# Linear attention's heads: output with tokens on the partitions, normalised by row sums, transposed afterwards

## The chip, the core and the metric

The kernel runs on one core of a Trainium2 chip. The metric is the device time of one execution in microseconds, the median of the runs shown. Engines are named as in the profile: PE is TensorE's matmul stream and PEld its weight loads, DVE is VectorE, ACT is ScalarE, POOL is GpSimd, SP is SyncE, which issues the DMAs.

## What is computed

A sequence of 512 tokens with 1024 features goes through four layers: sparse attention with an MLP, a convolution mixer with an MLP, a layer with a gated recurrence and a short convolution, and a gated linear attention layer. The change lies in the last one. Cut to what matters there:

```python
def odd_layer(x, norm_pre, norm_post, w_in, w_gate_lr, b_gate, head_norm_g, w_out):
    h = rmsnorm_2(x, norm_pre)
    q, k, v, r, lr = jnp.split(h @ w_in, [512, 1024, 2048, 3072], axis=-1)
    ...
    o_f = gla_chunked(qh, kh, vh, g_f)
    o_b = jnp.flip(gla_chunked(jnp.flip(qh, 2), jnp.flip(kh, 2), jnp.flip(vh, 2), jnp.flip(g_b, 2)), 2)
    o = rmsnorm_2(o_f + o_b, head_norm_g)
    o = jnp.transpose(o, (0, 2, 1, 3)).reshape(bsz, seq, GLA_VAL)
    y = (o * jax.nn.silu(r.astype(jnp.float32))) @ w_out
    return (x + rmsnorm_2(y, norm_post)).astype(x.dtype)
```

There are four heads with keys of 128 and values of 256 features. Each head's output, 512 tokens by 256 features, is the sum of a forward and a backward pass. It is normalised over the 256 features of each token, multiplied by a gain per feature (`head_norm_g`) and by silu(r), and goes into the last matrix product.

## The kernel before, in words

All large products are made in three matmuls of a rounded high part and a rest (`XH`, `XL` for the activations, `whi`, `wlo` for the weights, all fp32r, 512 columns each; lines 145 to 147 in `mac`). Weights come in chunks of 128 x 1024 by DMA into `stg`; ACT makes `whi` (L99) and DVE makes `wlo` (L100).

In the last layer the work of the heads is cut into steps: the generator `head(hd)` issues a few instructions and yields. The foreground is the stream of matmuls for `r` (eight output tiles `m`, each 24 matmuls) and then for `wod`, the last product. After every six matmuls of `r`, or every three of `wod`, `step` lets the background go on; which generator goes next is set by their place in a list `bg`, by credits, and by conditions at which a generator yields `WAIT`. So the order on every engine is fixed when the kernel is built, and a generator with another number of yields shifts all that come after it. All engines take their instructions in that order. After each tile `m`, DVE makes `rz` (L1567), ACT its sigmoid `sr` (L1569), POOL their product (L1570), and PE transposes a tile of the residual `h` (`hT`, L1552), which ACT copies back (L1553).

A head goes through these stages: scores `gsc` (L1408), masked by DVE into `Sm` (L1409) and added by POOL into `Sc` (L1411); transposed keys `ktT` (L1423); three rounds of `kv` (L1435), each followed by two `Z` on DVE (L1442, L1445) and two `U` on ACT (L1448), which are the states; and then the output, which the change rewrites.

The output stands with features on the partitions. For each half `eh` of the 256 features, one PSUM tile `go` of 128 x 512 holds all four blocks of 128 tokens, in ten matmuls of 128 columns:

```python
pe.matmul(o[:, pp], lhsT=vS[:, p, ec], rhs=Sc[:, p, :], start=True, stop=False)
if p > 0:
    pe.matmul(o[:, pp], lhsT=U[0, p][:, eu], rhs=E[hd, 0][0][:, pp], start=False, stop=p == 3)
if p < 3:
    pe.matmul(o[:, pp], lhsT=U[1, p][:, eu], rhs=E[hd, 1][0][:, pp], start=False, stop=True)
```

ACT squares the finished tile (`osq`, `sq`), POOL adds the two halves (L260), PE sums over the partitions by matmuls with a column of 1/256 (`om`, L267), ACT and DVE make the reciprocal root `rh` (L282, L283), four transposes spread it over the partitions (`spread`, L272), ACT copies it to `ori` (L274), DVE multiplies it and the gain on (`on`, L1493), and POOL, for the last head DVE, multiplies by `sr` (L1499). Then `tosplit` makes `XH` (L297) and `XL` (L298) from it for `wod`. PSUM tiles have tags: `a` with two buffers (`go`), `b` with two (`gsc`, `ktT`, `kv`), `c` with one (`om`, `spread`), `mm` with three (`r`, `hT`, `wod`).

Of the kernel before, what the change touches and what calls it, by code (L numbers as in the profile page):

```python
# [45 lines left out]
def tile_model(ctx, tc, xT, wall, gwall, vecs, opost, wglr, bglr, wdw, dft, out):  # L46
# [25 lines left out]
    def psum(tag, name):  # L72
        n = {"mm": 3, "a": 2, "b": 2, "c": 1}[tag]
        return ps.tile([P, NT], F32, tag=tag, name=name, bufs=n)
# [122 lines left out]
    def V(name, i=0, n=1):  # L197
        o = VEC[name] + i
        return vec[:, o:o + n]
# [41 lines left out]
    def tmp(name="t"):  # L241
        return tmp_pool[0].tile([P, NT], F32, tag="t", name=name, bufs=tmp_pool[1])
# [11 lines left out]
    def add_sq(k, src, acc, scale=1.0, eng=pool):  # L254
        if k == 0:
            act.activation(acc, src, AF.Square, scale=scale)
        else:
            t = tmp("sq")[:, :src.shape[-1]]
            act.activation(t, src, AF.Square, scale=scale)  # L259
            eng.tensor_tensor(out=acc, in0=acc, in1=t, op=ALU.add)  # L260
# [4 lines left out]
    def means(m, acc, col, scale_col, js=range(4)):  # L265
        for j in js:
            pe.matmul(m[:, col + j:col + j + 1], lhsT=acc[:, j * P:(j + 1) * P], rhs=scale_col, start=True, stop=True)  # L267
# [11 lines left out]
    def rsqrt_cols(dst, src):  # L279
        s = small("sd")  # L280
        n = src.shape[-1]
        act.activation(s[:, :n], src, AF.Sqrt, bias=eps)  # L282
        dve.reciprocal(dst, s[:, :n])  # L283
# [989 lines left out]
    with eo as e:  # L1273
# [20 lines left out]
        for d in range(2):  # L1294
# [11 lines left out]
            t = gp.tile([P, 4, P], F32, name=f"Sm{d}")  # L1306
            pool.memset(t, 0.0)
            Sm.append(t)
        ones256 = gp.tile([P, 1], F32, name="ones256")
        pool.memset(ones256, 1.0 / 256)  # L1310

        lro = psum("mm", "lr")
        hi, lo = weights()
# [84 lines left out]
        def head(hd):  # L1398
            while len(live) == 2:
                yield WAIT  # L1400
            live.append(hd)
            U = {}
            for d in range(2):
                qt, kt = E[hd, d]
                s = psum("b", "gsc")
                for p in range(4):
                    pp = slice(p * P, (p + 1) * P)
                    pe.matmul(s[:, pp], lhsT=kt[:, pp], rhs=qt[:, pp], start=True, stop=True)  # L1408
                dve.copy_predicated(Sm[d], mk[d], s.rearrange("p (a b) -> p a b", a=4))  # L1409
            Sc = hp.tile([P, 4, P], F32, tag="Sc", name="Sc", bufs=2)  # L1410
            pool.tensor_tensor(out=Sc, in0=Sm[0], in1=Sm[1], op=ALU.add)  # L1411
            yield
            while kb:
                yield WAIT
            kb.append(hd)
            order = [list(range(3)), list(range(3, 0, -1))]
            kts = []
            for d in range(2):
                kt = E[hd, d][1]
                t = psum("b", "ktT")  # L1420
                for p in order[d]:
                    pp = slice(p * P, (p + 1) * P)
                    pe.transpose(t[:, pp], kt[:, pp], ident)  # L1423
                k_ = hp.tile([P, NT], F32, tag="kTs", name="kTs", bufs=3)
                sl = slice(0, 3 * P) if d == 0 else slice(P, 4 * P)
                act.activation(k_[:, sl], t[:, sl], AF.Copy)
                kts.append(k_)
            yield
            yield
            Z = [None, None]  # L1430
            for i in range(3):
                kp = psum("b", "kv")
                for d in range(2):
                    p = order[d][i]
                    pe.matmul(kp[:, d * 256:(d + 1) * 256], lhsT=kts[d][:, p * P:(p + 1) * P], rhs=vS[:, p, hd * 256:(hd + 1) * 256], start=True, stop=True)  # L1435
                for d in range(2):
                    p = order[d][i]
                    gm = gam[hd, d]
                    kd = kp[:, d * 256:(d + 1) * 256]
                    zt = hp.tile([P, 256], F32, tag="Z", name="Z", bufs=4)  # L1440
                    if i == 0:
                        dve.tensor_copy(zt, kd)  # L1442
                    else:
                        q = order[d][i - 1]
                        dve.scalar_tensor_tensor(zt, Z[d], gm[:, q:q + 1], kd, op0=ALU.mult, op1=ALU.add)  # L1445
                    Z[d] = zt
                    ut = hp.tile([P, 256], F32, tag="U", name="U", bufs=12)
                    act.activation(ut, zt, AF.Copy, scale=gm[:, p:p + 1])  # L1448
                    U[d, p + 1 if d == 0 else p - 1] = ut
                if i == 2:  # L1450
                    kb.clear()
                    kvd.append(hd)
                yield
            while busy:
                yield WAIT
            busy.append(hd)
            for _ in range(2 if hd == 3 else 0):
                yield
            os_ = []
            sq = tmp("osq")  # L1460
            for eh in range(2):
                o = psum("a", "go")
                ec = slice(hd * 256 + eh * P, hd * 256 + (eh + 1) * P)
                eu = slice(eh * P, (eh + 1) * P)
                for p in range(4):
                    pp = slice(p * P, (p + 1) * P)
                    pe.matmul(o[:, pp], lhsT=vS[:, p, ec], rhs=Sc[:, p, :], start=True, stop=False)
                    if p > 0:
                        pe.matmul(o[:, pp], lhsT=U[0, p][:, eu], rhs=E[hd, 0][0][:, pp], start=False, stop=p == 3)
                    if p < 3:  # L1470
                        pe.matmul(o[:, pp], lhsT=U[1, p][:, eu], rhs=E[hd, 1][0][:, pp], start=False, stop=True)
                add_sq(eh, o, sq)
                os_.append(o)
                if eh:
                    live.remove(hd)
                yield
            yield
            for _ in range(2 if hd == 3 else 0):
                yield
            m = psum("c", "om")  # L1480
            means(m, sq, 0, ones256)
            rh = small("rh")
            rsqrt_cols(rh, m[:, 0:4])
            yield
            ri = tmp("ori")
            spread(ri, rh)
            yield
            while 2 * hd + 1 not in sr:
                yield WAIT
            on = []  # L1490
            for eh in range(2):
                t = tmp("on")
                dve.scalar_tensor_tensor(t, os_[eh], V("glg", eh), ri, op0=ALU.mult, op1=ALU.mult)  # L1493
                on.append(t)
            busy.clear()
            yield
            for eh in range(2):
                m = 2 * hd + eh
                (dve if hd == 3 else pool).tensor_tensor(out=sr[m], in0=on[eh], in1=sr[m], op=ALU.mult)  # L1499
                done.append(m)  # L1500
            yield

        done = []
        kvd = []
# [314 lines left out]
```

## Time and profile before

| | us |
|---|---|
| median of 3 runs | 1816.83 |
| lowest and highest | 1815.49, 1822.7 |
| the profiled execution, its own time | 1816.9 |
| its span, first to last instruction | 1815.2 |
| PE busy | 1785.0 |
| DVE, ACT, POOL busy | 979.1, 815.7, 442.5 |

The span is what the profile covers; the 1.7 us around it belong to the start and the end of the execution. Matmuls overlap in the pipeline, so a row's duration of one is longer than what it costs in a stream of them; the chain of waits shows the latter.

### The profile page before, as it was taken

The numbers are of one execution on the slowest core, as the hardware profiler recorded it, in microseconds if no ns is written. First come the engines' busy times: TensorE is split into PE (matmuls) and PEld (weight loads), VectorE is DVE, ScalarE is ACT, GpSimd is POOL, SyncE is SP. The second block draws the span as 40 slices with busy tenths as digits, with TensorE's granted clock in tenths as the row PEclk, the third lists the DMA queues.
The fourth block names the chain that finished last, engine by engine and source line by source line (L and its number), as shares of the span: only waits on it lengthen the run. The fifth ranks groups of instructions, "written<-read, shape, count | busy, mean of one in ns | idle before, by whom it ended". The sixth has DMA issues, their size and how long they took to land.

```text
span 1815.2 us, 22602 instructions
## 1 busy us (share of the span) xinstructions
PE 1785.0 (98%) x8796; PEld 1490.1 (82%) x8796; DVE 979.1 (54%) x1430; ACT 815.7 (45%) x1267; POOL 442.5 (24%) x380
## 2 busy tenths in 40 slices
PE   9999999999999999999999999999999999999998
PEld 7778878888888878898888888888887888888887
DVE  4796544333333658765333333786677743756354
ACT  5334444332323434564332323558666734456553
POOL 1333422010202202436010202412313103552330
PEclk9999999999999999999999999999999999999999
DMA  5222113223232233112323222232322233222121
GB/s 191 70 71 81 47 59 104 94 93 104 93 104 93 82 103 105 47 40 78 105 93 104 87 100 94 81 116 95 100 96 76 91 112 104 72 99 70 47 71 47
DMA packets 45931, 159.68 MB, mean 88 GB/s; under 512 B 5217, under 2 KB 6625, under 8 KB 45824
## 3 DMA queue, kind: packets, MB, share of 16 engines
q1 hardware_dynamic: 45824, 158.24, 26.1%
q8 instruction: 69, 1.13, 0.3%
q14 instruction: 38, 0.31, 0.1%
HBM read 156.13 MB, written 2.10 MB: 87 GB/s over the span
## 4 chain that ended last, share of the span: by engine, by line
PE 88%; DVE 5%; ACT 3%; issue 2%; DMA 1%; POOL 0%; SPq 0%; DVEq 0%; ACTq 0%; POOLq 0%
PE w L146 12%; PE w L147 12%; PE w L145 12%; PE ko L146 2%; PE ko L147 2%; PE ko L145 1%; PE a L145 1%; PE a L147 1%; PE a L146 1%; PE k L145 1%; PE lg L467 1%; PE o L499 1%; ACT whi L99 1%; PE v L441 1%; PE q L147 1%
## 5 line engine op out<-in xcount | busy, mean ns | idle before, releaser
L100 DVE TENSOR_TENSOR wlo<-stg,whi 128x1024 fp32r<-128x1024 f32 x247 | 328.5, 1332 | 267.5 <-ACT whi L99 266.4
L99 ACT ACTIVATE whi<-stg 128x1024 fp32r<-128x1024 f32 x284 | 297.6, 1051 | 222.5 <-PE w L146 125.4
L596 POOL TENSOR_TENSOR UL<-u,UH 128x512 fp32r<-128x512 f32 x64 | 83.5, 1305 | 514.5 <-ACT UH L595 514.5
L145 PE MATMUL w<-XH,whi 128*128 128x512 f32 (+1 forms) x520 | 200.7, 386 | 0.0
L146 PE MATMUL w<-XL,whi 128*128 128x512 f32 (+1 forms) x520 | 200.7, 386 | 0.0
L147 PE MATMUL w<-XH,wlo 128*128 128x512 f32 (+1 forms) x520 | 200.7, 386 | 0.0
L146 PE MATMUL w<-UL,whi 128*128 128x512 f32 x512 | 199.5, 390 | 0.1
L147 PE MATMUL w<-UH,wlo 128*128 128x512 f32 x512 | 199.3, 389 | 0.0
L145 PE MATMUL w<-UH,whi 128*128 128x512 f32 x512 | 199.3, 389 | 0.0
L100 POOL TENSOR_TENSOR wlo<-stg,whi 128x1024 fp32r<-128x1024 f32 x37 | 89.6, 2428 | 122.1 <-ACT whi L99 121.9
L260 POOL TENSOR_TENSOR sacc<-sacc,sq 128x512 f32<-128x512 f32 (+1 forms) x57 | 71.0, 1253 | 182.4 <-ACT sq L259 118.3
L147 PEld LDWEIGHTS w<-XH,wlo 128*128 128x128 f32 x520 | 97.7, 188 | 19.7
L145 PEld LDWEIGHTS w<-XH,whi 128*128 128x128 f32 x520 | 97.7, 188 | 19.7
L146 PEld LDWEIGHTS w<-XL,whi 128*128 128x128 f32 x520 | 97.7, 188 | 19.6
L146 PEld LDWEIGHTS w<-UL,whi 128*128 128x128 f32 x512 | 96.1, 188 | 20.9 <-POOL UL L596 1.0
L145 PEld LDWEIGHTS w<-UH,whi 128*128 128x128 f32 x512 | 96.1, 188 | 20.0
L147 PEld LDWEIGHTS w<-UH,wlo 128*128 128x128 f32 x512 | 96.1, 188 | 19.9
L592 ACT ACTIVATE relu<-w 128x512 f32<-128x512 f32 x64 | 38.2, 597 | 151.8 <-PE w L147 151.8
L594 DVE TENSOR_TENSOR u<-relu 128x512 f32<-128x512 f32 x64 | 45.4, 709 | 104.5 <-ACT relu L592 104.5
L146 PE MATMUL ko<-XL,whi 128*128 128x256 f32 x256 | 74.6, 291 | 3.8 <-DVE XL L252 2.2
L145 PE MATMUL ko<-XH,whi 128*128 128x256 f32 x256 | 75.5, 295 | 2.4 <-ACT XH L823 2.4
L604 DVE TENSOR_TENSOR acc<-w,acc 128x512 f32<-128x512 f32 x32 | 22.1, 691 | 97.0 <-PE w L147 97.0
(485 smaller groups left out, 4101.1 us busy)
## 6 DMA issues: line engine op xcount, KB each, us to landing
stg<-wall SPq DMA_DIRECT2D x284, 512.0 KB, 3.3
gst<-gwall SPq DMA_DIRECT2D x4, 512.0 KB, 3.6
h<-xT SPq DMA_DIRECT2D x3, 512.0 KB, 6.2
out<-yo SPq DMA_DIRECT2D x6, 256.0 KB, 2.1
stg<-wall SPq DMA_DIRECT2D x8, 128.0 KB, 5.2
h<-xT SPq DMA_DIRECT2D x2, 256.0 KB, 4.1
ex<-wglr SPq DMA_DIRECT2D x2, 256.0 KB, 2.7
sacc<-opost SPq DMA_DIRECT2D x2, 256.0 KB, 4.4
```

What stands on the lines that cost most here:

```text
L99: act.activation(hi, src, AF.Copy)
L100: eng.tensor_tensor(out=lo, in0=src, in1=hi, op=ALU.subtract)
L145: pe.matmul(o, lhsT=hi[:, w], rhs=xh[:, k, ns], start=first, stop=False)
L146: pe.matmul(o, lhsT=hi[:, w], rhs=xl[:, k, ns], start=False, stop=False)
L147: pe.matmul(o, lhsT=lo[:, w], rhs=xh[:, k, ns], start=False, stop=last)
L260: eng.tensor_tensor(out=acc, in0=acc, in1=t, op=ALU.add)
L441: pe.matmul(acc[t], lhsT=XH[:, k, xs], rhs=wh, start=k == 0, stop=False)
L467: pe.matmul(l[:, :w], lhsT=qh[hd][:, j * P:(j + 1) * P], rhs=kT[:, hd, :w], start=True, stop=True)
L592: act.activation(r, o, AF.Relu)
L594: dve.tensor_tensor(out=u, in0=r, in1=r, op=ALU.mult)
L596: pool.tensor_tensor(out=UL[:, m, :], in0=u, in1=UH[:, m, :], op=ALU.subtract)
L604: dve.tensor_tensor(out=a, in0=o, in1=a, op=ALU.add)
```

## The change

The output of a head is now made with tokens on the partitions. For each block p of 128 tokens the operands change places: `Sc` and the decayed queries are the stationary ones, `vS` and `U` the moving ones with all 256 features, so a block is one product of 128 x 256. Blocks 0 and 1 lie side by side in one `go` tile, blocks 2 and 3 in another. ACT squares each block and sums along the row with it (`accum_out`), which gives `ss`; ACT takes the root and DVE the reciprocal (`rh`), and the four blocks are scaled by it into `on`, blocks 0 and 2 on ACT, 1 and 3 on DVE. Then, for each half of the features, PE transposes four times into a tile `onT` (tag `c`), and DVE multiplies by the gain and by `sr` in one instruction. The sums by POOL, `om`, `spread`, `ori` and the products on POOL are gone, and the yields of the generator stand at other places.

```diff
-            os_ = []
-            sq = tmp("osq")
-            for eh in range(2):
-                o = psum("a", "go")
-                ...
-                add_sq(eh, o, sq)
-                os_.append(o)
-                if eh:
-                    live.remove(hd)
-                yield
-            yield
-            for _ in range(2 if hd == 3 else 0):
-                yield
-            m = psum("c", "om")
-            means(m, sq, 0, ones256)
+            os_ = [psum("a", "go") for _ in range(2)]
+            ss = small("ss")
+            dv = slice(hd * 256, (hd + 1) * 256)
+            outs = [os_[p // 2][:, (p % 2) * 256:(p % 2) * 256 + 256] for p in range(4)]
+            for p in range(4):
+                pp = slice(p * P, (p + 1) * P)
+                o = outs[p]
+                pe.matmul(o, lhsT=Sc[:, p, :], rhs=vS[:, p, dv], start=True, stop=False)
+                if p > 0:
+                    pe.matmul(o, lhsT=E[hd, 0][0][:, pp], rhs=U[0, p], start=False, stop=p == 3)
+                if p < 3:
+                    pe.matmul(o, lhsT=E[hd, 1][0][:, pp], rhs=U[1, p], start=False, stop=True)
+                act.activation(tmp("osq")[:, :256], o, AF.Square, accum_out=ss[:, p:p + 1])
+                if p == 3:
+                    live.remove(hd)
+                if p % 2:
+                    yield
+            yield
             rh = small("rh")
-            rsqrt_cols(rh, m[:, 0:4])
-            yield
-            ri = tmp("ori")
-            spread(ri, rh)
+            act.activation(rh, ss, AF.Sqrt, scale=1.0 / 256, bias=eps)
+            dve.reciprocal(rh, rh)
+            on = [tmp("on") for _ in range(2)]
+            for p in range(4):
+                w = on[p // 2][:, (p % 2) * 256:(p % 2) * 256 + 256]
+                if p % 2:
+                    dve.tensor_scalar(w, outs[p], rh[:, p:p + 1], None, op0=ALU.mult)
+                else:
+                    act.activation(w, outs[p], AF.Copy, scale=rh[:, p:p + 1])
+            busy.clear()
             yield
             while 2 * hd + 1 not in sr:
                 yield WAIT
-            on = []
+            for _ in range(2 if hd == 3 else 1):
+                yield
             for eh in range(2):
-                t = tmp("on")
-                dve.scalar_tensor_tensor(t, os_[eh], V("glg", eh), ri, op0=ALU.mult, op1=ALU.mult)
-                on.append(t)
-            busy.clear()
-            yield
-            for eh in range(2):
+                t = psum("c", "onT")
+                for p in range(4):
+                    pe.transpose(t[:, p * P:(p + 1) * P], on[p // 2][:, (p % 2) * 256 + eh * P:(p % 2) * 256 + eh * P + P], ident)
                 m = 2 * hd + eh
-                (dve if hd == 3 else pool).tensor_tensor(out=sr[m], in0=on[eh], in1=sr[m], op=ALU.mult)
+                dve.scalar_tensor_tensor(sr[m], t, V("glg", eh), sr[m], op0=ALU.mult, op1=ALU.mult)
                 done.append(m)
-            yield
+                yield
```

Three places of the built order, each before and after; a bracket names the engines whose semaphores an instruction waits for. First PE at head 0's output, blocks of the first group (`vS` are the values, `Sc` the scores, `U` the states, `qk` and `qkb` the decayed queries forward and backward). Before:

```order
L1467 MATMUL go<-Sc,vS_12498 128x128 [waits Pool_49]
L1471 MATMUL go<-qkb_12441,U 128x128 [waits Activation_49]
L1467 MATMUL go<-Sc,vS_12498 128x128
L1469 MATMUL go<-qk_12440,U 128x128
L1471 MATMUL go<-qkb_12441,U 128x128
```

After, the same place, lines 1465 to 1469 of the changed kernel:

```order
L1465 MATMUL go<-vS_12498,Sc 128x256 [waits Pool_49]
L1469 MATMUL go<-U,qkb_12441 128x256 [waits Activation_49]
L1465 MATMUL go<-vS_12498,Sc 128x256 [waits Activation_49]
L1467 MATMUL go<-U,qk_12440 128x256
L1469 MATMUL go<-U,qkb_12441 128x256
```

The third matmul, the first of block 1, now waits for ACT, and the matmuls are half as many with twice the columns.

Second ACT around the second half of head 2's output, while the keys of head 3 are worked on (`XH` is the high part of a finished head's tile). Before, where `sq` is that half's square:

```order
L99 ACTIVATE whi<-stg 128x1024 [waits DMAHW5_49]
L297 ACTIVATE XH<-sr 128x512 [waits PE_49]
L259 ACTIVATE sq<-go 128x512 [waits PE_49,Activation_49]
L297 ACTIVATE XH<-sr 128x512
L297 ACTIVATE XH<-sr 128x512 [waits Pool_49]
L1569 ACTIVATE sr<-rz 128x512 [waits DVE_49]
```

After, where the two `osq,ss` are that half's squares:

```order
L1567 ACTIVATE sr<-rz 128x512 [waits DVE_49]
L1551 ACTIVATE h<-hT 128x512 [waits PE_49]
L99 ACTIVATE whi<-stg 128x1024 [waits DMAHW6_49]
L1446 ACTIVATE U<-Z,gm_12981 128x256 [waits DVE_49]
L1446 ACTIVATE U<-Z,gm_12964 128x256 [waits DVE_49]
L297 ACTIVATE XH<-sr 128x512
L99 ACTIVATE whi<-stg 128x1024 [waits DMAHW7_49]
L99 ACTIVATE whi<-stg 128x1024 [waits DMAHW0_49]
L1446 ACTIVATE U<-Z,gm_12981 128x256 [waits DVE_49]
L1446 ACTIVATE U<-Z,gm_12964 128x256 [waits DVE_49]
L1470 ACTIVATE osq,ss<-go 128x256 [waits PE_49]
L1470 ACTIVATE osq,ss<-go 128x256 [waits PE_49,Pool_49]
```

The squares moved from ahead of the last `sr` to behind it, behind two pairs of `U` and three `whi`.

Third DVE in the same stretch. Before:

```order
L1567 TENSOR_TENSOR rz<-r,rs 128x512 [waits PE_49]
L100 TENSOR_TENSOR wlo<-stg,whi 128x1024 [waits DMAHW6_49,Activation_49]
L283 RECIPROCAL rh<-sd 128x4 [waits Activation_49]
L298 TENSOR_TENSOR XL<-sr,XH 128x512 [waits Activation_49]
L100 TENSOR_TENSOR wlo<-stg,whi 128x1024 [waits DMAHW7_49,Activation_49]
L100 TENSOR_TENSOR wlo<-stg,whi 128x1024 [waits DMAHW0_49,Activation_49]
```

After:

```order
L1565 TENSOR_TENSOR rz<-r,rs 128x512 [waits PE_49]
L100 TENSOR_TENSOR wlo<-stg,whi 128x1024 [waits DMAHW6_49,Activation_49]
L1443 SCALAR_TENSOR_TENSOR Z<-Z,gm_12981,kv 128x256 [waits DVE_49,PE_49]
L1443 SCALAR_TENSOR_TENSOR Z<-Z,gm_12964,kv 128x256 [waits DVE_49]
L298 TENSOR_TENSOR XL<-sr,XH 128x512 [waits Activation_49]
L100 TENSOR_TENSOR wlo<-stg,whi 128x1024 [waits DMAHW7_49,Activation_49]
L100 TENSOR_TENSOR wlo<-stg,whi 128x1024 [waits DMAHW0_49,Activation_49]
L1443 SCALAR_TENSOR_TENSOR Z<-Z,gm_12981,kv 128x256 [waits DVE_49,PE_49]
L1443 SCALAR_TENSOR_TENSOR Z<-Z,gm_12964,kv 128x256 [waits DVE_49]
```

The `Z` of head 3's second and third round, which stood behind all of this, now stand between the `wlo`.

## Rows read from the trace of the kernel before

**Rows 1.** The page's first part: busy us (share of the span) and instructions by engine.
```profile
PE 1785.0 (98%) x8796; PEld 1490.1 (82%) x8796; DVE 979.1 (54%) x1430; ACT 815.7 (45%) x1267; POOL 442.5 (24%) x380
```
**Rows 2.** The page's fourth part: shares of the chain that ended last, by engine.
```profile
PE 88%; DVE 5%; ACT 3%; issue 2%; DMA 1%; POOL 0%; SPq 0%; DVEq 0%; ACTq 0%; POOLq 0%
```
**Rows 3.** Who waited for whom, 1670 to 1816 us: total, times, longest.
```profile
DVE yo L1626 <- ACT junk L1625: 13.4, 9, 3.3
...
PE spread L272 <- DVE rh L283: 1.0, 1, 1.0
...
PE wod L1583 <- ACT XH L297: 0.4, 1, 0.4
...
PE gsc L1408 <- DVE Z L1445: 0.3, 1, 0.3
...
PE go L1467 <- DVE on L1493: 0.2, 1, 0.2
```
**Rows 4.** The chain that ended last in order of time, 1700 to 1722 us: start, us.
```profile
1702.55 0.23 PE r L146
...
1703.70 0.79 PE om L267 x8
...
1706.00 0.86 PE kv L1435 x4
...
1708.26 0.45 PE spread L272 x4
...
1719.53 1.78 PE gsc L1408 x16
```
**Rows 5.** PE's timeline: start, us from first start to last end, count of records.
```profile
1682.15 1.03 PE L1435 MATMUL kv<-vS,kTs 128*128 128x256 f32 x4
...
1752.36 0.60 PE L1552 MATMUL hT<-ident,h 128*128 128x128 f32 x4
...
1809.19 0.28 PE L1585 MATMUL wod<-whi,XL 128*128 128x256 f32 x1
```
**Rows 6.** Timelines of ACT and DVE at the tail, 1800 to 1816 us.
```profile
1803.80 0.60 ACT L1625 ACTIVATE junk<-wod 128x512 f32<-128x512 f32 x1 [4.52 <-PE wod L1585]
...
1809.57 0.38 ACT L1625 ACTIVATE junk<-wod 128x256 f32<-128x256 f32 x1 [2.44 <-PE wod L1585]
1809.85 0.19 ACT L1625 ACTIVATION_READ_ACCUMULATOR junk<-wod 128x1 f32 x1
...
1810.08 0.42 DVE L1626 TENSOR_TENSOR yo<-wod,sacc 128x256 f32<-128x256 f32 x1 [2.42 <-ACT junk L1625]
```
**Rows 7.** Timelines of DVE and ACT, 1752 to 1770 us.
```profile
1752.99 0.68 DVE L1567 TENSOR_TENSOR rz<-r,rs 128x512 f32<-128x512 f32 x1
1755.79 1.23 DVE L100 TENSOR_TENSOR wlo<-stg,whi 128x1024 fp32r<-128x1024 f32 x1 [2.13 <-ACT whi L99]
...
1758.83 2.36 DVE L100 TENSOR_TENSOR wlo<-stg,whi 128x1024 fp32r<-128x1024 f32 x2 [0.26 <-ACT whi L99]
...
1768.15 0.87 DVE L1445 SCALAR_TENSOR_TENSOR Z<-Z,gm,kv 128x256 f32<-128x256 f32 x2 [0.75 <-PE kv L1435]
...
1757.23 0.62 ACT L297 ACTIVATE XH<-sr 128x512 fp32r<-128x512 f32 x1
1757.75 2.00 ACT L99 ACTIVATE whi<-stg 128x1024 fp32r<-128x1024 f32 x2
...
1768.67 0.91 ACT L1448 ACTIVATE U<-Z,gm 128x256 f32<-128x256 f32 x2 [0.68 <-DVE Z L1445]
```
**Rows 8.** DVE's timeline at head 0's reciprocal root.
```profile
1707.10 0.18 DVE L283 RECIPROCAL rh<-sd 128x4 f32<-128x4 f32 x1 [0.35 <-ACT sd L282]
```
**Rows 9.** Three stretches: length, busy us by engine, then PE's granted clock, DMA share, GB/s.
```profile
1555.73:1557.63 1.90, 0.01 (x2) 0.03 (x1) 1.75 (x1) 1.20 (x2) 1.90 (x2) 1.00 0.00 0
1561.53:1563.47 1.94, 0.00 (x1) 0.00 (x1) 1.94 (x3) 0.81 (x2) 1.60 (x2) 1.00 0.58 192
1563.94:1567.35 3.41, 3.41 (x19) 3.41 (x18) 3.34 (x7) 1.08 (x3) 1.31 (x2) 0.50 0.31 120
```

More of the change, by code (lines that the diff above doesn't have):

```diff
@@ L1308, in tile_model @@
             Sm.append(t)
-        ones256 = gp.tile([P, 1], F32, name="ones256")
-        pool.memset(ones256, 1.0 / 256)
         lro = psum("mm", "lr")
@@ L1458, in head @@
                 yield
-            os_ = []
-            sq = tmp("osq")
-            for eh in range(2):
-                o = psum("a", "go")
[L1463 to L1471, printed above, removed]
-                add_sq(eh, o, sq)
-                os_.append(o)
-                if eh:
+            os_ = [psum("a", "go") for _ in range(2)]
```

## The prediction

> **What bounds the kernel now.** I read the page first. TensorE (PE) is busy 98% of the span, the other engines half or less [rows 1], and the chain that ended last is 88% PE [rows 2]. So what PE issues, and what it waits for, sets the time. The change lies in the output part of the four heads, which runs between about 1670 and 1790 us, in between the matmuls of `r` (heads 0 to 2) and of `wod`. For that stretch I read who waited for whom: PE waited four times, 1.9 us in all [rows 3]. It is bound by PE's own stream, then, with almost no time lost: work taken from PE is gained nearly in full, and each new wait of PE is paid nearly in full. ACT and DVE are half idle, but each takes its queue in order, and those few waits of PE are for work of theirs that came a fraction late.
>
> The sum below is made against the profiled execution, 1816.9 us (span 1815.2); the median of the runs shown is 1816.83, so both stand at the same place.
>
> **PE's own work.** Matmuls of 128 columns in f32 cost PE 0.223 us each: the sixteen records of `gsc`, two to a matmul, take 1.78. Two matmuls of 256 columns (`kv`) take 0.86, so 0.43 each; the four of `om` take 0.79, the four transposes of `spread` 0.45 [rows 4]. Per head, before: twenty `go` of 128 columns, 4.46, and 0.79 and 0.45, together 5.70. After: ten of 256 columns, 4.30, and eight transposes `onT`, 0.90, together 5.20. Half a microsecond per head, for four heads **-2.0 us**. Columns are what is paid here, so halving the number of matmuls gives next to nothing.
>
> **The new wait inside a bank.** Token blocks 0 and 1 now share one 512-column PSUM tile, as do 2 and 3, and ACT squares block 0 before PE is given block 1. In the built order the first matmul of block 1 carries a wait for ACT, and so does that of block 3: two per head, eight in all. Before, a `go` matmul waited for U, or at the start of a group, and never in between. So PE now stands still while ACT reads. The price comes from the tail, where ACT squares and sums 256 columns right after PE: PE's last matmul ends at 1809.47 [rows 5], the square starts at 1809.57, its accumulator has been read out at 1810.04, and the DVE that waited for it starts at 1810.08 [rows 6]. That is 0.61 us from PE's end to the next engine. And a matmul ends later than its slot: the records of `kv` end 1.03 after they start [rows 5] but take 0.86 of PE's time [rows 4], 0.17 more. So 0.78 each, eight times: **+6.2 us**, if ACT is free. Bounds: 0 if the halves of a bank are independent; 1.0 each if the square cost what one of 512 columns does, 0.60 for 0.38 [rows 6].
>
> What the trace leaves open is whether two halves of a bank need that wait at all. A row shows DVE waiting for ACT on `wod` banks nine times, 13.4 us [rows 3], but there both read the same columns; by that row alone the term could still be 0. The Trainium skill (PSUM — Partial Sum Buffer, section "PSUM bank collisions raise a hardware error") says "Semaphore-guard PSUM by **bank × quadrant** (by bank is the simple version), not by address". By that rule any columns of the bank count, and all eight waits are due; no run here shows one yet.
>
> **Where ACT is late.** In the new order the second half of head 2 stands behind all three `kv` of head 3 on PE. Its first square stands on ACT behind U, U, XH, whi, whi, U, U, and those wait for DVE, where rz, wlo, Z, Z, XL, wlo, wlo, Z, Z stand. Laid out with the rows: from rz's start to the end of its wlo 4.03 us (1752.99 to 1757.02); Z, Z, U, U 1.43 (1768.15 to 1769.58); from XH to the end of the second of two wlo 3.96 (1757.23 to 1761.19) [rows 7]; Z, Z, U, U again 1.43; the square with its read-out and the way to PE 0.51 [rows 6]. Together 11.4 us, and rz starts 0.6 after PE came to the four hT behind the last `r` (1752.36) [rows 5, 7]. PE has until then four hT (0.45), fifteen `wod` matmuls of 0.23 like those of `r` [rows 4] (3.45), two `kv` pairs (1.72) and three `go` (1.29), 6.9 us. So it waits 11.4 + 0.6 - 6.9 = 5.1, of which 0.8 is counted above: **+4.3 us**. Bounds 2 and 6: nine pieces, each of which may overlap a little or come later.
>
> **Head 1's start.** Its first `go` moves up to where head 0's `spread` stood, and needs the bank that head 0's `on` reads. Before, rh began at 1707.10 [rows 8], and PE came to `spread` at 1708.26 [rows 4]; without `om`, and a little less in `go`, that is about 1707.3. Now come one after the other, since ACT and DVE read one bank: rh 0.18 [rows 8], `on` of block 0 on ACT 0.38, of block 1 on DVE 0.42 (both as the 256-column reads of the tail) [rows 6], so the bank is free at 1708.1: 0.8 of waiting. Then `on` of block 3, 0.42, and Z, Z, U, U 1.43 [rows 7]: U is there at 1709.9, while the second matmul could have started at 1708.5: 1.4 more. **+2.2 us**, bounds 0.5 and 3.
>
> **Head 3's second transposes.** `onT` has one PSUM buffer, so the four for the second half wait until DVE has multiplied the first out, and two wlo stand before that on DVE, 2.36 [rows 7]; the product takes 0.7, as rz does [rows 7], and 0.6 passes until the first whi is there: ACT makes it after its last `on` in 1.0 (two take 2.00) [rows 7], while DVE has 0.42 of its own to do. On PE only nine `wod` matmuls and the first four transposes lie between, 2.07 + 0.45. **+1.2 us**, bounds 0 and 2.
>
> **What costs nothing.** POOL loses four sums of squares and six products for `sr`; at 24% busy [rows 1] it bounds nothing, and the matmuls of `r` and `wod` covered those products. They cover DVE's new pass as well; where that cover is thin, at head 3, its cost is the term above. The four waits of before belong to the old order; in the new one a wlo, an XH or a Z will again be late by a fraction somewhere, so I leave the 1.9 us standing [rows 3], bounds -1.9 and +2. The order of the DMAs is the same.
>
> **The clock.** PE paused 1.90 us, and 4 us later 1.94 us; the granted clock then stood at 0.50, that is 1.2 GHz, for 3.41 us, which loses 1.7 us of full speed [rows 9]. A pause of 5 us is longer than both, so I count one such fall after it: **+1.7 us**, bounds 0 and 5 (a second one after head 1's waits, or a longer one).
>
> Sum: -2.0 + 6.2 + 4.3 + 2.2 + 1.2 + 1.7 = +13.6; 1816.9 + 13.6 = **1830.5 us**.
>
> **Rivals.**
> *The halves are independent*, and PE never stops between blocks: -2.0, and with head 1's 2.2 back or not, 1814.9 to 1817.1, no change that can be measured. For it: the columns differ. Against: the built order has the wait, and ACT raises its semaphore only after the read-out. It turns on one thing, whether PE idles between blocks 0 and 1. Chance 0.06.
> *Only the round trips*: ACT reaches head 2's square in time, and the clock holds: -2.0 + 6.2 + 2.2, 1823.3, within 0.5%. For it: ACT is 45% busy [rows 1]. Against: its queue is in order, and what it waits for is DVE's. Chance 0.11.
> *The clock falls more than once*: head 1's pauses, some 3 us within 4, look like the two in [rows 9]. Two or three falls instead of one: 1832 to 1834. Chance 0.18.
> *The forecast*: 0.65.
>
> **From these to the numbers.** 0.5% is 9.1 us (about what a measurement of this kernel can tell from no change), so the line lies at 1825.9. With the pair wait at 0.6, the late square at its low bound and no fall of the clock the forecast still gives 1825; with its high bounds for the late square, the onT and the clock, 1836. The round trips alone end at 1823. Leaving out the independent halves and the far ends, the range is 1822 to 1836. Slower by over 0.5%: 0.82 (the clock rival and nearly all of the forecast); within 0.5%: 0.16 (the other two rivals, nearly); faster: 0.02.
>
> **What would show it.** In the changed profile: `go` of 256 columns at 0.43 us each; eight waits of PE's `go` for the square on ACT, seven near 0.8 and one near 5, at about 1770; one or two waits at head 1's first `go`; a granted clock of 0.50 for a few us after the long one; POOL without sums and products. If no `go` waits for the square, or the long wait is under 1 us, the forecast is wrong; so it is if all waits are there and the time is not, since then they took the place of others that I counted as work.

## The result, and the profile after

The changed kernel takes **1831.97 us** (median of 4 runs, 1830.33 to 1832.6), beside 1817.19 for the kernel before on the same chip (4 runs): a ratio of 1.0082, 95% interval 1.0068 to 1.0096, so 14.8 us slower. A second set of 4 runs gave 1831.27 beside 1816.82 (1.0072, 1.0051 to 1.0093). Forecast were 1830.5, 13.6 more than before.

First the page of the changed kernel (profiled execution 1830.33, span 1828.6), its first part and the engines' shares of the chain that ended last.

```profile
PE 1788.2 (98%) x8700; PEld 1486.5 (81%) x8700; DVE 978.0 (53%) x1436; ACT 819.6 (45%) x1295; POOL 427.8 (23%) x369
...
PE 87%; DVE 5%; ACT 4%; issue 2%; DMA 1%; POOL 0%; SPq 0%; DVEq 0%; ACTq 0%; POOLq 0%
```

Beside [rows 1, 2] almost nothing has moved: PE still at 98%, with 96 of its records fewer (40 matmuls and transposes; an f32 matmul leaves two records). A share rounded to per cents can't show 14 us in 1800; a reader who stops here finds no cause. The waits show it. Who waited for whom, 1670 to 1830 us, changed kernel: total, times, longest.

```profile
PE go L1465 <- ACT osq L1470: 8.9, 8, 4.6
PE go L1465 <- DVE on L1483: 1.1, 1, 1.1
PE onT L1495 <- DVE sr L1497: 1.0, 1, 1.0
PE go L1469 <- ACT U L1446: 1.0, 1, 1.0
PE gsc L1406 <- DVE Z L1440: 0.5, 1, 0.5
```

Where [rows 3] had 1.9 us, there are now 12.9 (two waits of `wod`, 0.2 each, are left out above). The first line is the new wait inside a bank: eight times, one of them 4.6. PE's timeline shows each; the bracket is the idle time after PE's modelled end, and what ended it.

```profile
1689.10 0.59 PE L1469 MATMUL go<-U,qkb 128*128 128x256 f32 x2
1690.25 0.70 PE L1465 MATMUL go<-vS,Sc 128*128 128x256 f32 x2 [0.56 <-ACT osq L1470]
1690.79 0.59 PE L1467 MATMUL go<-U,qk 128*128 128x256 f32 x2
1691.22 0.59 PE L1469 MATMUL go<-U,qkb 128*128 128x256 f32 x2
...
1707.55 0.40 PE L147 MATMUL r<-XH,wlo 128*128 128x512 f32 x1
1709.09 0.67 PE L1465 MATMUL go<-vS,Sc 128*128 128x256 f32 x2 [1.14 <-DVE on L1483]
1710.71 0.70 PE L1469 MATMUL go<-U,qkb 128*128 128x256 f32 x2 [0.96 <-ACT U L1446]
...
1762.90 0.59 PE L1469 MATMUL go<-U,qkb 128*128 128x256 f32 x2
1768.07 1.22 PE L1465 MATMUL go<-vS,Sc 128*128 128x256 f32 x2 [4.58 <-ACT osq L1470]
...
1796.71 0.66 PE L1495 MATMUL onT<-ident,on 128*128 128x128 f32 x4 [1.05 <-DVE sr L1497]
```

Read the starts, not the brackets: a matmul of 256 columns takes 0.43 in a stream (1690.79 to the next at 1691.22), so from 1689.10 to 1690.79 there should be 0.86, and there are 1.69. The stop costs 0.83: the 0.56 of the bracket, the 0.17 by which a matmul outlasts its slot, and about 0.1 because the first one after a stop takes 0.54. Over the seven ordinary stops that difference is 0.83, 0.83, 0.89, 1.04, 0.84, 0.89 and 0.84, in all 6.2, or 0.88 each.

The long stop, at head 2's second half: timelines of ACT and DVE in the changed kernel.

```profile
1762.37 0.61 ACT L297 ACTIVATE XH<-sr 128x512 fp32r<-128x512 f32 x1
1762.89 1.99 ACT L99 ACTIVATE whi<-stg 128x1024 fp32r<-128x1024 f32 x2
1766.75 0.91 ACT L1446 ACTIVATE U<-Z,gm 128x256 f32<-128x256 f32 x2 [1.87 <-DVE Z L1443]
1767.57 0.36 ACT L1470 ACTIVATE osq<-go 128x256 f32<-128x256 f32 x1
1767.83 0.19 ACT L1470 ACTIVATION_READ_ACCUMULATOR osq<-go 128x1 f32 x1
...
1757.09 0.68 DVE L1565 TENSOR_TENSOR rz<-r,rs 128x512 f32<-128x512 f32 x1
...
1763.97 2.36 DVE L100 TENSOR_TENSOR wlo<-stg,whi 128x1024 fp32r<-128x1024 f32 x2 [0.26 <-ACT whi L99]
1766.24 0.87 DVE L1443 SCALAR_TENSOR_TENSOR Z<-Z,gm,kv 128x256 f32<-128x256 f32 x2
```

Block 2 was finished by 1763.5. Its square, for which PE stood, took ACT half a microsecond; but it stands behind `U`, which waits for `Z`, which stands on DVE behind two `wlo`, which wait for `whi` on ACT. ACT idled 1.87 us in front of `U` with a square ready behind it. From `rz` to PE's next matmul 11.0 us went by; the prediction laid out 11.4.

Last the clock behind that stop. Stretches of the changed kernel: length, busy us by engine, PE's granted clock, DMA share, GB/s.

```profile
1764.30:1767.68 3.38, 0.00 (x0) 0.00 (x0) 2.81 (x4) 1.51 (x4) 0.00 (x0) 1.00 0.42 122
1767.68:1771.09 3.41, 3.02 (x7) 2.47 (x8) 0.00 (x0) 1.17 (x5) 0.00 (x0) 0.50 0.08 32
1771.09:1780.00 8.91, 8.61 (x38) 5.87 (x37) 3.94 (x7) 3.33 (x6) 0.00 (x0) 1.00 0.00 0
```

The granted clock was 0.50, that is 1.2 GHz, for 3.41 us; PE worked in 3.02 of them and lost half, 1.5 us.

### The profile page after: what moved, and what is told of

Same layout as the page of the kernel before. It is cut to its first block, busy times and chain, and to the rows that moved or that the text cites. A ratio compares the mean times of both kernels' runs of the same rounds, so it can differ in the third digit from the quotient of the medians.

```text
span 1828.6 us, 22431 instructions
## 1 busy us (share of the span) xinstructions
PE 1788.2 (98%) x8700; PEld 1486.5 (81%) x8700; DVE 978.0 (53%) x1436; ACT 819.6 (45%) x1295; POOL 427.8 (23%) x369
## 4 chain that ended last, share of the span: by engine, by line
PE 87%; DVE 5%; ACT 4%; issue 2%; DMA 1%; POOL 0%; SPq 0%; DVEq 0%; ACTq 0%; POOLq 0%
PE w L146 12%; PE w L147 12%; PE w L145 12%; PE ko L146 2%; PE ko L147 2%; PE ko L145 2%; PE a L145 1%; ACT whi L99 1%; PE a L147 1%; PE a L146 1%; PE k L145 1%; PE lg L467 1%; PE o L499 1%; PE v L441 1%; PE q L147 1%
## 5 line engine op out<-in xcount | busy, mean ns | idle before, releaser
L592 ACT ACTIVATE relu<-w 128x512 f32<-128x512 f32 x64 | 38.2, 597 | 151.7 <-PE w L147 151.7
L147 PE MATMUL ko<-XH,wlo 128*128 128x256 f32 x256 | 74.3, 290 | 0.0
```

The source lines that it names most:

```text
L147: pe.matmul(o, lhsT=lo[:, w], rhs=xh[:, k, ns], start=False, stop=last)
L592: act.activation(r, o, AF.Relu)
```

## A measure of the stage alone

PE's instructions ahead of the heads are the same in all kernels, and times of whole executions vary with how long they take. So for each profile I also read a stretch of the last layer alone. Read from the start of the layer's first matmul, of `lr` (it makes the gates' low-rank input), to the end of the last of `wod`, it is 204.02 us before and 218.43 after; the expectations of the last two experiments mean this stretch where they say the first matmul of `r`. But it holds a wait that has nothing to do with the heads: ahead of `r`, PE's `spread` waits for `rc` on DVE. Who waited for whom, 1605 to 1669 us, before and in the second experiment:

```profile
PE spread L272 <- DVE rc L283: 0.2, 1, 0.2
PE spread L272 <- DVE rc L283: 1.3, 1, 1.3
```

In the eighth experiment it is absent. The 300 records of PE between `lr` and `r` are the same in every kernel and take 64.7 to 66.2 us, 64.9 without this wait wherever there is one. So the stage below is the stretch from the start of the first matmul of `r` (at 1670.60 in the kernel before) to the end of the last of `wod`. Before, and after:

```profile
1670.60:1809.47 138.87, 136.96 (x785) 117.77 (x783) 64.10 (x99) 62.81 (x112) 29.96 (x22) 1.00 0.16 54
```

```profile
1669.69:1822.90 153.21, 140.18 (x689) 112.94 (x687) 63.22 (x105) 66.75 (x140) 15.38 (x12) 0.99 0.15 49
```

The stage is 14.3 us longer. In the table below, "PE at 0.50" is PE's busy time in the stretches with a granted clock of 0.50 inside the stage, and "at full clock" is a stretch less half of that.

| kernel | time, us | ratio to before (95%) | from `lr` | PE at 0.50 | from `lr` at full clock | stage at full clock |
|---|---|---|---|---|---|---|
| before | 1816.83 | | 204.02 | 0 | 204.0 | 138.9 |
| changed | 1831.97 | 1.0082 (1.0068 to 1.0096) | 218.43 | 3.02 | 216.9 | 151.7 |
| changed, second set | 1831.27 | 1.0072 (1.0051 to 1.0093) | 221.10 | 8.13 | 217.0 | 151.6 |
| squares after both blocks | 1826.13 | 1.0053 (1.0038 to 1.0068) | 213.88 | 9.10 | 209.3 | 143.3 |
| the same at head 2 alone | 1829.85 | 1.0071 (1.0054 to 1.0088) | 219.53 | 6.82 | 216.1 | 149.9 |
| neighbours in two banks | 1823.61 | 1.0036 (1.0023 to 1.0049) | 211.82 | 6.55 | 208.5 | 142.7 |
| before, tile squared in halves | 1822.46 | 1.0034 (1.0021 to 1.0047) | 210.74 | 0 | 210.7 | 144.8 |
| matmuls into the pause | 1830.03 | 1.0064 (1.0040 to 1.0088) | 217.37 | 0 | 217.4 | 152.2 |
| two banks and other steps | 1816.33 | 0.9999 (0.9990 to 1.0008) | 204.50 | 0 | 204.5 | 139.1 |
| other steps alone | 1826.14 | 1.0054 (1.0040 to 1.0067) | 211.79 | 0 | 211.8 | 147.1 |
| two banks and other steps, again | 1817.32 | 1.0001 (0.9989 to 1.0012) | 204.57 | 0 | 204.6 | 139.2 |
| other steps alone, again | 1824.66 | 1.0041 (1.0026 to 1.0055) | 212.43 | 0 | 212.4 | 147.1 |

## The experiments

The theory: PE stops inside a bank, eight times for a round trip to ACT, and once for a late ACT. Rivals: the stops take the place of waits that PE would have anyway; the lateness of ACT does it alone; what the change adds and moves (other steps, transposes, DVE's pass) costs in itself. Line numbers in the experiments' rows stand one to four higher than in the changed kernel where an edit adds lines.

**1. Squares after both blocks.** ACT squares blocks 0 and 1 only when PE has been given both:

```diff
-                act.activation(tmp("osq")[:, :256], o, AF.Square, accum_out=ss[:, p:p + 1])
+                if p % 2:
+                    for b in (p - 1, p):
+                        act.activation(tmp("osq")[:, :256], outs[b], AF.Square, accum_out=ss[:, b:b + 1])
```

> Only change against the changed kernel: ACT squares blocks 0 and 1 after PE has been given both (2 and 3 likewise). My theory: the eight waits of go for the square go away. Their idle in the changed kernel was 8.9 us, 4.6 of it in head 2, and 0.17 each more by the pipeline's end, so about 10 us. But the late square of head 2 is late for what follows it too: root, scaling and then the transposes onT stand only 15 wod matmuls (3.4 us) behind, so a wait of about 3 us appears at onT. Expect 1824.5 (1822.5 to 1826.5), about +7 against the kernel before. Rival A, the order of the steps costs the time and the waits only show it: 1830 to 1832. Rival B, the waits were all of it and nothing follows: 1819 to 1820.

Measured: 1826.13; the stage 143.3 at full clock, 8.4 below the changed kernel. Who waited for whom on PE:

```profile
PE onT L1497 <- ACT on L1487: 3.0, 1, 3.0
```

No `go` waits for a square any more, and 8.9 us of waits became a new one of 3.0: the transposes of head 2, which wait for `on` on ACT. The time lies at the upper end of what was expected: PE worked longer at 0.50 here, 9.10 us, which cost 4.5.

**2. The same at head 2's second half alone**, where the long stop was.

```diff
-                act.activation(tmp("osq")[:, :256], o, AF.Square, accum_out=ss[:, p:p + 1])
+                late = hd == 2 and p > 1
+                if not late or p % 2:
+                    for b in (p - 1, p) if late else (p,):
+                        act.activation(tmp("osq")[:, :256], outs[b], AF.Square, accum_out=ss[:, b:b + 1])
```

> The same, but for the second half of head 2 alone; the other seven waits stay. My theory: its wait of 4.6 us goes, but some 3 us of it comes back at the transposes onT of head 2, so only 1.5 to 2 us are gained: 1830 (1829 to 1831.5), with a wait of about 3 us of PE for ACT's or DVE's on. If the clock no longer falls after the shorter pause, 1.7 less: 1828.3. Rival: the late square costs only because of the shared bank, so 4.8 us and the fall of the clock are gained: 1825.5.

Measured: 1829.85, in the expected range; stage 149.9, only 1.8 below the changed kernel at full clock, though the longest wait of all, 4.6, is gone. PE's waits:

```profile
PE go L1465 <- ACT osq L1473: 4.3, 7, 0.8
PE onT L1498 <- ACT on L1488: 3.0, 1, 3.0
```

And the timelines of PE and ACT at the place:

```profile
1767.37 0.59 PE L1465 MATMUL go<-vS,Sc 128*128 128x256 f32 x2
1767.80 0.59 PE L1467 MATMUL go<-U,qk 128*128 128x256 f32 x2
1774.80 0.33 PE L1498 MATMUL onT<-ident,on 128*128 128x128 f32 x1 [2.96 <-ACT on L1488]
...
1770.78 0.91 ACT L1446 ACTIVATE U<-Z,gm 128x256 f32<-128x256 f32 x2 [1.87 <-DVE Z L1443]
1771.60 0.36 ACT L1473 ACTIVATE osq<-go 128x256 f32<-128x256 f32 x1
...
1772.43 1.28 ACT L1480 ACT_TABLE_LOAD   x1
...
1774.27 0.84 ACT L1488 ACTIVATE on<-go,rh 128x256 f32<-128x256 f32 x2 [0.24 <-DVE rh L1481]
```

PE runs on at 1767.37 and stops fifteen matmuls of `wod` later. ACT's queue is as late as before (`U`, then the squares, the load of the table for the root, the root, `on`), and the transposes hang on its end. The 4.3 us that the prediction put down to "ACT is late" were real as a wait, but most of them were not to be had by taking this wait away.

**3. Neighbouring blocks in different banks.** Everything stays, but blocks 0 and 2 share one tile, 1 and 3 the other:

```diff
-            outs = [os_[p // 2][:, (p % 2) * 256:(p % 2) * 256 + 256] for p in range(4)]
+            outs = [os_[p % 2][:, (p // 2) * 256:(p // 2) * 256 + 256] for p in range(4)]
```

> Only change against the changed kernel: blocks 0 and 2 share one PSUM tile, 1 and 3 the other; the order of instructions stays. My theory: no go waits for the square of the block before it any more, since that one lies in the other bank; also DVE's on no longer waits for ACT's, which shortens head 1's wait by some 0.4 us. Otherwise as with the squares after both: 1823.5 (1821.5 to 1826). Rival: the wait is not due to the bank (the queues or the stationary operands make it): no change, 1831 to 1832.

Measured: 1823.61, stage 142.7, 9.0 below the changed kernel. Where PE still waits:

```profile
PE onT L1495 <- ACT on L1485: 3.0, 1, 3.0
PE onT L1495 <- DVE sr L1497: 1.4, 1, 1.4
PE go L1465 <- ACT on L1485: 1.0, 1, 1.0
```

Not one `go` waits for a square. The order of the instructions is the changed kernel's, the columns that ACT reads and PE writes were different ones in both kernels; only the bank differs. The Trainium skill's rule (PSUM — Partial Sum Buffer, section "PSUM bank collisions raise a hardware error") to guard PSUM by bank and not by address is what the program does: eight waits with a shared bank, none here. Whether the chip itself would have got by without them was not tried: by that rule such a kernel would have a race.

**4. The kernel before, with the same stop and nothing else of the change.** ACT squares the first 256 columns of each `go` tile after block 1, so that PE has to stop ahead of block 2:

```diff
+                    if p == 1:
+                        add_sq(eh, o[:, :256], sq[:, :256])
-                add_sq(eh, o, sq)
+                add_sq(eh, o[:, 256:], sq[:, 256:])
```

> The kernel before, with one thing of the change added: in each go tile (features on the partitions, as before) ACT squares the first 256 columns after block 1, before PE writes blocks 2 and 3 into the other half of that bank. POOL adds the halves apart. My theory: eight round trips of 0.65 to 0.8 us, ACT being free at each: +5 to +6.5, so 1822.2 to 1823.7. Rival: the shared bank costs nothing in itself, the transposed layout and its order do: 1817 to 1818.

Measured: 1822.46, stage 144.8, 5.9 above before. PE's waits:

```profile
PE go L1467 <- ACT osq L256: 2.1, 4, 0.5
PE go L1467 <- ACT sq L259: 2.0, 4, 0.5
PE spread L272 <- DVE rh L283: 0.6, 1, 0.6
```

Eight stops of 0.5 in the brackets; from start to start the matmuls of `go` take 6.2 us longer in all, 0.78 for each stop. The price of a round trip stands by itself, here without an accumulator to be read out and without any other part of the change. These stops take the place of next to nothing: PE's four waits of before are still there, and only that of `spread` for `rh` is shorter, 0.6 instead of 1.0.

**5. Work into the long pause.** The changed kernel, with 18 matmuls of 128 columns ahead of the last block of head 2's `go`; nobody reads what they write.

```diff
+                if hd == 2 and p == 3:
+                    hot = psum("c", "hot")
+                    for _ in range(18):
+                        pe.matmul(hot[:, :P], lhsT=ident, rhs=ident, start=True, stop=True)
```

> The changed kernel, with 18 matmuls of 128 columns that nobody reads put on PE into its long pause (before the block that waits for head 2's late square). They cost 18 x 0.223 = 4.0 us of PE and fit into the pause of 4.6. My theory: the pause is hidden work for PE's clock, and the time is lost twice, by the wait and by the clock that falls after it; with PE busy the clock stays at full speed there, and this kernel with more work is FASTER by 1.7 us: 1830.3 where the changed kernel stands at 1832.0, with no granted clock of 0.50 near 1768 us. Rival A, the clock doesn't matter or falls anyway: the same as the changed kernel. Rival B, the matmuls delay something: up to 4 us more.

Measured: 1830.03, in the same set of runs as the changed kernel's 1831.27. The intervals overlap, so the times alone settle nothing: neither a gain of 1.7 nor "the same as the changed kernel" is excluded. The stretch around the pause:

```profile
1763.00:1769.00 6.00, 5.44 (x43) 5.11 (x42) 3.84 (x5) 3.90 (x8) 0.00 (x0) 1.00 0.52 169
1769.00:1776.00 7.00, 6.89 (x30) 5.07 (x31) 2.16 (x5) 3.53 (x7) 0.00 (x0) 1.00 0.00 0
```

The clock stays at 1.00, and no other stretch of the stage is at 0.50. Four microseconds more work on PE (18 by 0.22) cost 0.5 to 0.6 at full clock, 152.2 against 151.7 and 151.6. In this one profile with work in the pause, and in the two without, the pause and the fall go together; one profile can't exclude that the fall stayed away by chance.

**6. The changed kernel once more**, for a second profile:

> The changed kernel once more on the same chip, as the measure for the run with the busy pause: 1830 to 1833. By my theory its executions differ by whole falls of the clock, 1.7 us each: where the granted clock is 0.50 near 1768 alone the time is about 1830.3, and where it also falls at head 1's waits (near 1710) about 1832.

Measured: 1831.27; the profiled execution 1833.84 with the waits of the first one to within 0.1. Only the clock differs: stretches of this execution.

```profile
1714.06:1717.47 3.41, 3.41 (x9) 2.58 (x9) 0.00 (x0) 1.76 (x3) 0.00 (x0) 0.50 0.00 0
1768.68:1775.51 6.83, 4.72 (x11) 3.79 (x12) 1.32 (x4) 3.54 (x9) 0.00 (x0) 0.50 0.25 77
```

Behind head 1's two waits a fall that the first profile didn't have, and behind the long one a fall twice as long. PE worked 8.13 us at 0.50 instead of 3.02, which cost 2.6 more; the stages differ by 2.5, and at full clock they agree within 0.1. One and the same program, so, draws one fall or more.

**7. Two banks and other steps.** The banks of 3, and other numbers of yields, so that what is late stands later: none ahead of head 3's first `go`, two or three ahead of the root, other numbers between the halves and ahead of the transposes, by head.

```diff
-            for _ in range(2 if hd == 3 else 0):
+            for _ in range((0, 0, 0, 0)[hd]):
...
-                if p % 2:
+                for _ in range((1, 1, 0, 1)[hd] if p == 1 else 0):
                     yield
-            yield
+            for _ in range((2, 3, 2, 2)[hd]):
+                yield
...
+            for _ in range((0, 0, 0, 1)[hd]):
+                yield
             busy.clear()
...
-            for _ in range(2 if hd == 3 else 1):
+            for _ in range((0, 2, 1, 2)[hd]):
                 yield
```

> The changed kernel with neighbouring blocks in different banks and, besides, other places of the heads' yields (head 2's two halves in one step, so before the keys of head 3; more steps between the squares and the root, and ahead of the transposes). My theory: what is left of the change once its waits are gone is PE's own work, 2.0 us less than before, and some 4 us of small waits against the 1.9 us before; no long pause, so no fall of the clock in the heads. Expect 1817 (1815 to 1819), the same as the kernel before. Rival: something in the layout itself is dear (row sums on ACT, scaling, transposes), and it stays at 1821 or more.

Measured: 1816.33 beside 1816.25, a ratio of 0.9999 (0.9990 to 1.0008): no difference from the kernel before. PE's waits, and then the row of the stage:

```profile
PE onT L1498 <- ACT on L1486: 1.7, 2, 1.1
PE kv L1433 <- DVE Z L1440: 1.0, 1, 1.0
PE go L1469 <- ACT U L1446: 0.5, 1, 0.5
```

```profile
1669.45:1808.55 139.10, 135.60 (x689) 112.75 (x687) 63.08 (x105) 67.19 (x140) 15.71 (x12) 1.00 0.16 54
```

The output with tokens on the partitions, the transposes and DVE's pass are all still there, and cost nothing on balance (139.1 beside 138.9): what made the change slow is where it stands, in the banks and in the order. Nothing is gained over before either. Here 3.6 us of waits are left (with two of 0.2 at `wod`), 1.7 more than before, and that is about what PE's own work is less.

**8. The other steps alone**, with blocks 0 and 1 in one bank again.

```diff
-            outs = [os_[p % 2][:, (p // 2) * 256:(p // 2) * 256 + 256] for p in range(4)]
+            outs = [os_[p // 2][:, (p % 2) * 256:(p % 2) * 256 + 256] for p in range(4)]
```

> The same places of the yields, but neighbouring blocks in one bank as in the changed kernel. My theory: no late square any more, so all eight waits are plain round trips of 0.73 to 0.8 us: 6 to 7 us above the version with different banks, 1823.5 (1822 to 1826). Rival: with better places of the steps the shared bank costs nothing: the same as the other.

Measured: 1826.14, 9.8 above the seventh, and just over the expected range. The waits show no late ACT at a square, and eight short stops:

```profile
PE go L1465 <- ACT osq L1470: 5.0, 8, 0.8
PE onT L1498 <- ACT on L1486: 1.7, 2, 1.1
PE onT L1498 <- DVE on L1484: 0.4, 2, 0.2
```

And the stage:

```profile
1671.95:1819.04 147.09, 138.20 (x689) 112.13 (x687) 63.00 (x105) 67.19 (x140) 15.71 (x12) 1.00 0.15 51
```

In the stage that is 8.0 us above the seventh. From start to start the matmuls of `go` take 7.2 us longer, 0.90 per stop; 0.9 more comes at the transposes, which twice wait for DVE's `on` as well, and that waits for ACT's `on`, which reads the same bank: 2.2 us in four waits, none of them in the seventh. The two profiled executions are 10.5 apart; the other 2.5 lay ahead of the stage, which begins at 1671.95 instead of 1669.45.

With the changed kernel and the third run this makes four versions: a stage of 151.7 as changed, 142.7 with the banks alone, 147.1 with the steps alone, 139.1 with both. So the banks are worth 9.0 or 8.0 us and the steps 4.6 or 3.6, depending on which comes first, and together they take back 12.6 of the 12.8 that the change cost.

**9. The seventh and the eighth again, side by side**, to see whether that rest belongs to the edit.

> The same kernel as in the run on banks and steps, to see what of the 9.8 us between it and the one with the same steps and the shared bank lies in this layer. From the first matmul of r to the last of wod its first profile took 204.5 us, with no fall of the clock in it. Both theories: 204.5 again, and a time of 1816 to 1817.

> The same kernel as in the run on the steps alone. Its first profile took 211.8 us from the first matmul of r to the last of wod, 7.3 more than with neighbouring blocks in different banks; the other 2.5 to 3 us lay in the layers before, whose code is the same, where the clock stood at 0.50 for 6.8 us longer in its profile. Theory: those are falls of the clock that come and go by execution; then the stage takes 211.8 again, and the time comes out 7 to 8 us above the run with the banks (1823.5 to 1825). Rival: the shared bank's kernel draws more falls in the layers before in every execution; then the gap stays near 9.8 us (1826), and its profile shows again some 7 us more at 0.50 before 1600 us than the other's.

Measured: 1817.32, just over the 1816 to 1817 expected, and 1824.66, 7.3 apart, in the range of the theory; the stages 139.2 and 147.1, 8.0 apart as the first time. The rival is weakened and not gone: this profile of the eighth again stood at 0.50 in the layers ahead for 10.2 us longer than the seventh's, after 6.8 the first time (the stage begins at 1674.12 instead of 1669.70; the execution took 1828.67, above the median of 1824.66), and the medians of its two sets, 1826.14 and 1824.66, differ. Why a kernel whose layers ahead are the same should draw more of them stays open. The cost of the shared bank in the stage, 8.0 both times, does not hang on it.

## Why the prediction was right

The sign, the mechanism and the size held: +13.6 forecast, +14.8 and +14.5 measured; 1831.97 lies in the range, 1.5 above the forecast. Its terms against the profile after, in us:

| term | forecast | measured | from |
|---|---|---|---|
| PE's own work | -2.0 | about -1.5 | seventh run: stage 139.1 less 3.6 of waits, before 138.9 less 1.9 |
| new wait inside a bank, 8 | +6.2 | +7.0 | 0.88 each over seven stops |
| where ACT is late | +4.3 | +4.0 | 1768.07 less 1762.90 less 0.43, and 0.1 for the restart as at the other stops, is 4.84; less 0.88 |
| head 1's start | +2.2 | +2.6 | 1.31 and 1.08 between slots, and 0.1 twice |
| head 3's second transposes | +1.2 | +1.2 | 1.05 in the bracket, and 0.17 |
| the waits of before | 0 | -1.0 | 0.9 left (`gsc` 0.5, two of `wod`) of 1.9 |
| the clock | +1.7 | +1.5 and +4.1 | two executions |

The terms without the clock add up to 12.3; the stage at full clock grew by 12.8, so half a microsecond has no row. Forecast were 11.9 without the clock. Each of these terms holds to 1.0 us or better. In part they cancel, which is luck: the stops cost 0.8 more and PE's own work fell by 0.5 less than forecast, and against that the waits of before, which the forecast left standing, went by half. Head 3's term was added up a tenth too high: its pieces, 2.36 + 0.7 + 0.6 less 2.52, make 1.1.

*The price of a stop* was mis-sized by a tenth, from 0.78 to 0.88. The chain from PE's end to the next engine was right: the brackets, 0.56 in four of seven, with 0.17 give 0.73. What was missing is that PE's first matmul after a stop takes 0.54 of its time rather than 0.43, and that three stops, where ACT came a little later, have 0.62 to 0.77 in the bracket.

*Where ACT is late* came out within 0.3, from nine pieces laid end to end, and the total 11.0 for 11.4. But as a statement on the cause it was too simple: the second experiment takes this wait away and gains 1.8, since PE's next need of the same late chain through ACT and DVE, the transposes, then waits 3.0.

*Independent halves* (0.06) fell: eight waits, and 6.2 us for the stops alone in the fourth run. That rests on the program's waits, not on what the chip would do without them. *Only the round trips* (0.11) fell by the 4.58 in PE's timeline. *The clock falls more than once* (0.18) and the forecast were no alternatives: the same program did the one in the first profile and the other in the second. The runs, 1829.6 to 1833.8, hold both. The median, 1831.97, lies nearer to this rival's 1832 than to the forecast's 1830.5; how many falls the executions without a profile drew is not known.

All the signs named beforehand were there: `go` at 0.43, eight waits for the square, seven near 0.8 and one near 5 at 1768, two waits at head 1, a granted clock of 0.50 behind the long one, and POOL at 427.8 instead of 442.5.

## What to carry to other kernels

Where PE bounds a kernel, a reader put between two groups of matmuls in one PSUM bank stops PE for the whole round trip, here 0.8 to 0.9 us each time on average, even if the columns are others, as the program guards whole banks; putting neighbouring groups into different banks cost nothing here and took it away. A long wait in a profile is worth what is left when the next consumer of the same late queue has had its turn: follow the queue to its end before booking the gain. And where moving work shifts the order of in-order queues, separate the two in the measurement: here the arithmetic was neutral, and the banks (8 to 9 us) and the order (about 4) made nearly the whole difference.

## What was not expected of the hardware

PE's clock varied between executions of one program with the same waits: one stretch at 0.50 of 3.41 us in one, 10.24 us in all in the other, and times 3.5 us apart (1830.33 and 1833.84). Four microseconds of unread matmuls in PE's pause left the stage at full clock 0.5 to 0.6 longer and the clock at 1.00. And the first matmul after a stop of half a microsecond, at a granted clock of 1.00, took 0.54 of PE's time instead of 0.43.
